# Moving scan work and one filler unit around the seams of a two-layer DiT kernel on one core

## The chip, the cores and the metric

The kernel runs on one core of a Trainium2 chip, in one launch. Five engines work side by side, each through its own queue in order: TensorE (PE; its weight loads are listed as PEld), VectorE (DVE), ScalarE (ACT), GpSimd (POOL) and SyncE (SP), which issues DMAs here; POOL issues DMAs too. The metric is the device time of one execution in microseconds; the median of several runs counts.

## The reference

One sequence of 256 tokens (`x`) and a context of 256 tokens (`ctx`), both 2048 wide, go through two layers in float32. All 18 arrays are inputs; the weights are read from memory once per run.

```python
h = _rmsnorm(x, norm_g[i]) * (1 + scale) + shift          # shift, scale, gate = silu(c) @ ada_w[i] + ada_b[i]
# layer 0: Fourier mixer, for x and for ctx
u, z = jnp.split(h @ w_in, 2, axis=-1)                    # 2 x 4096 wide
f = jnp.fft.fft2(ug, axes=(1, 3), norm='ortho').real      # 16 groups of 256
y = einsum('bngc,gcd->bngd', f, w_mix) * silu(z)
# layer 1: attention of x over itself and ctx
q, k, v, z = jnp.split(h @ w_in, [4096, 4608, 5120], axis=-1)   # 64 query heads, 8 key/value heads of 64
s = (q @ k.T) * 64 ** -0.5, masked to a window of 128, plus all of ctx
p = softmax(concat([s, sink]))[..., :-1]
y = (p @ v) * silu(z)
# both layers
x = x + gate * (y @ w_out[i])
# at the end
out = _rmsnorm(x, final_g)
```

## The kernel before

Products are made at nearly float32 accuracy from pairs: a value is split into a high part (a cast on ACT) and a low part (a subtraction on DVE or POOL), and `mm3` (lines 145 to 147) issues three matmuls, high by high, high by low and low by high. Two kinds of pairs are used, f16 (`split16`, lines 137 and 138) and fp32r (`split`, lines 66 and 67). The f16 kind needs scale factors so that nothing overflows; they are taken from sums of squares of the weights. For that reason the kernel reads the later weights ahead, in pieces of 128x1024 (512 KB), and squares and sums each piece, while earlier stages run. "Scan" means this reading and squaring in what follows.

The stages, in the order of time: the opening (norm and transform of x, and adaLN products) and the Fourier groups; the z product of layer 0 (32 blocks); layer 0's output product, a loop of 32 tiles (`i`, two sweeps of 16 for the two halves of the columns), in which the remaining adaLN sums are made on DVE too; norm and keys and values of layer 1 (8 weight blocks `kg`); the attention loop; and the output product of layer 1 with the final norm.

The pools that matter: `raw` (3 slots of 1 MB for weights as they land), `ws` (6 slots for split weights), `act` (33 slots of 128x512 float32), and 8 banks of PSUM, `ps`. A pool `kvp` lives through the keys' and values' stage; the pool `at` of the attention loop opens when it has closed. `h1` has 16 slots for layer 1's input and, later, for the parts of its output y.

The scan in layer 0's output product. `scan_loads1(n)` (called with `w_rate[i]` at tile `i`) issues n pieces, each as two loads of 256 KB into `act` slots, on POOL's queue (line 821 holds such a load). `scan_sums()` squares on ACT (line 829) what is pending, at the next tile. At tile 28 `h1_bound()` reduces the sums that the scale factors of the next stage need, and turns them through memory (two small DMAs on POOL); `h1_scale()` at tile 31 makes the factors. At tiles 12 to 15 and 28 to 31 POOL also loads x for the residual, and POOL's queue then holds the constants of layer 1: rope, mask and sinks (line 60). `ada_rate` gives the number of adaLN steps a tile takes.

The scan in the keys' and values' stage. `loads2(n)` issues pieces into four slots `pz` of `kvp`, 35 in all, over steps 0 to 11 (two steps per weight block); `sums2()` (lines 1177 and 1179) squares what is pending on ACT or on DVE. A last `sums2(True)` takes what is left once the stage's products are out of PSUM, and line 1235 reduces the 35 sums into one. The products leave PSUM through copies on ACT (1224 and 1225 for the values and their absolute values, 1231 for the context's keys) and the rotation on DVE (`roped`, 1132 to 1138). The values' own scale comes from a small product of ones with their absolute values (line 1238), then lines 1240 to 1254 make the f16 pair of the values: a product on DVE (1252), a cast on ACT (1253), a subtraction on POOL (1254).

The attention loop. All weight products of layer 1's queries, z and the first of its output rows are cut into units of one 128x1024 half block: 8 units for each of 8 groups of query heads ("q"), 2 for each of 32 z blocks ("z"), and 14 "o" units, each two of the 32 steps of k of the first 512 output columns. `emit_unit()` prepares the weights of the next unit and issues the products of the current one; `filler()` calls it and may issue a postponed transposition of queries. 10 units come ahead of the loop. Then, for each head `i`: scores, mask and softmax (`stage_s`, 1489 to 1509; the mask and the maximum are one DVE instruction, line 1491; the high and low f16 parts of the probabilities are lines 1506 on ACT and 1507 on DVE; DMAs on SP's queue transpose them, line 1509), a filler, the product with the values of head `i - 2` (`stage_o`, 1524 and 1525), and another filler. The last o steps, k = 28 to 31, are left for `first_rest()` in the stage after the loop, and the parts of y for them lie in the pool `fin`.

What sets the order. Tile's planner goes over the whole program once, simulates the engines, and writes each engine's queue: among the instructions that are ready by its own times it takes the one that the program names first. Program order is thus a priority and not the order itself. `tc.issue_after(x)` ties what stands inside it behind x on x's engine.

Of the kernel before, what the change touches and what calls it, by code (L numbers as in the profile page):

```python
# [11 lines left out]
F32R = mybir.dt.float32r  # L12
F16 = mybir.dt.float16
AF = mybir.ActivationFunctionType
ALU = mybir.AluOpType
AX = mybir.AxisListType

P = 128
# [3 lines left out]
NB = DB // P  # L22
# [10 lines left out]
def tile_dit(ctx: ExitStack, tc: tile.TileContext, a: dict, out: bass.AP):  # L33
    nc = tc.nc
    V, S, PE, GP = nc.vector, nc.scalar, nc.tensor, nc.gpsimd
# [8 lines left out]
    def psum():  # L44
        return pp.tile([P, 512], F32, tag="ps", name="ps")
# [9 lines left out]
    def act(dt=F32):  # L55
        return actp.tile([P, 512], dt, tag="act", name="act")
# [8 lines left out]
    def split(h, l, src, eng=V):  # L65
        last_cast[0] = S.copy(h, src).ins  # L66
        last_sub[0] = eng.tensor_tensor(l, src, h.bitcast(F32), op=ALU.subtract).ins  # L67
# [76 lines left out]
    def mm3(o, wh, wl, xh, xl, start, stop):  # L144
        PE.matmul(o, wh, xh, start=start, stop=False)  # L145
        PE.matmul(o, wh, xl, start=False, stop=False)  # L146
        return PE.matmul(o, wl, xh, start=False, stop=stop).ins  # L147
# [491 lines left out]
    for g in range(G):  # L639
        for j in {13: (8, 9), 14: (10, 11)}.get(g, (g - 5,) if 5 <= g < 13 else ()):  # L640
            t = up.tile([P, 1024], F32, name="pz", tag="pz", bufs=1)
# [164 lines left out]
    scn = adat.tile([P, 108], F32, name="scn")  # L806
# [5 lines left out]
    yq = adab[:, 1, 0].rearrange("p k s -> p (k s)")  # L812
# [46 lines left out]
    with tc.tile_pool(name="yp", reuse_waits="tile", bufs=32) as ypool:  # L859
        ys = []  # L860
# [38 lines left out]
        if True:  # L899
# [21 lines left out]
            for kg in range(4):  # L921
# [10 lines left out]
                for j in range(4):  # L932
                    k = kg * 4 + j
# [66 lines left out]
        identr = act(F32R)[:, 0:P]  # L1000
        S.copy(identr, ident)
        ada_rate = {**{i: 2 for i in (*range(6, 10), *range(17, 26))}, **{i: 0 for i in (14, 15, 16, 28, 29, 30, 31)}}
        w_rate = {10: 1, 11: 1, 14: 2, 15: 2, 16: 2, 17: 1, 18: 1, 20: 1, 22: 1, 24: 1, 26: 2, 27: 2, 28: 3, 29: 2, 30: 1}
        hbd = dram.tile([P, 2], F32, name="hbd")
        hb1 = []

# [24 lines left out]
        for i in range(32):  # L1031
# [26 lines left out]
            if kg >= 12:  # L1058
                for k in range(sw * 8 + (kg - 12) * 2, sw * 8 + (kg - 12) * 2 + 2):
                    t = act()  # L1060
# [79 lines left out]
    with tc.tile_pool(name="h1", reuse_waits="tile", bufs=16) as h1p:  # L1140
# [4 lines left out]
        with tc.tile_pool(name="kvp", reuse_waits="tile", bufs=2) as kvp:  # L1145
# [4 lines left out]
            for k in range(KT):  # L1150
                z2 = kvp.tile([P, 1024], F16, tag="hz", name="hz", bufs=16)
                t = kvp.tile([P, 512], F32, tag="ht", name="ht")
# [18 lines left out]
            scn = kvp.tile([P, 35], F32, name="scn", bufs=1)  # L1171

            def sums2(act_only):
                for n in range(len(pend)):
                    t, c = pend.pop(0)
                    if n < 2 or act_only:
                        S.activation(t, t, AF.Square, accum_out=c)
                    else:
                        V.tensor_tensor_reduce(t, t, t, 1.0, 0.0, ALU.mult, ALU.add, c)
# [16 lines left out]
            for kg in range(8):  # L1196
# [16 lines left out]
                for j in range(2):  # L1213
                    k = kg * 2 + j
# [7 lines left out]
            for tb in range(4):  # L1222
                t, ab = act(), act(F32R)
# [3 lines left out]
                t = act()  # L1227
# [3 lines left out]
                    S.activation(t, o[tb][0], AF.Copy, scale=dnk)  # L1231
                kr.append(t)

            sums2(True)
            V.tensor_reduce(yq[:, 17:18], scn, axis=AX.X, op=ALU.add)
            l1 = psum()
            for tb in range(4):
                PE.matmul(l1, oner, vs[tb][1], start=tb == 0, stop=tb == 3)
# [9 lines left out]
            for tb in range(4):  # L1248
                t = vs[tb][0]
                va = actp.tile([P, 8, P], F16, tag="act", name="v")  # L1250
                tv = t.rearrange("p (h d) -> p h d", d=64)
                V.tensor_tensor(t, t, up_, op=ALU.mult)
                S.copy(va[:, :, 0:64], tv)
                GP.tensor_tensor(va[:, :, 64:128], tv, va[:, :, 0:64], op=ALU.subtract)
                v01.append(va)

        y1 = []
        raw1, fin = [None], []
        oA, kg1, yh = [], [0], []
        with tc.tile_pool(name="at", reuse_waits="tile", bufs=2) as at:  # L1260
# [4 lines left out]
            def w1_next():  # L1265
                n = kg1[0]
                kg1[0] += 1
                if n % 2 == 0:
                    raw1[0] = raw(a["wo1a"][n // 2])
                return half_split(raw1[0], n % 2)  # L1270

            def y_split(k):
                t = (h1p if k < 28 else fin[0]).tile([P, 512], F32R, tag="h1" if k < 28 else "ys", name="ys", bufs=16 if k < 28 else 4)
                split(t[:, 0:N], t[:, N : 2 * N], y1[k // 2][:, (k % 2) * N : (k % 2 + 1) * N], GP if k < 24 else V)
                yh.append(t)

# [3 lines left out]
            def y_sums(n, i):  # L1280
                while ynext[0] < min(n, len(ypairs)) and ypairs[ynext[0]] <= i - 2:
                    j = ynext[0]
                    ynext[0] += 1
                    S.activation(act(), y1[j], AF.Square, accum_out=yq[:, j : j + 1])

            def out_scale():
                V.tensor_reduce(yq[:, 18:19], yq[:, 0:14], axis=AX.X, op=ALU.add)
                o = psum()
                for c, i, st in ((0, 16, True), (0, 17, False), (1, 18, True)):
                    PE.matmul(o[:, c : c + 1], ones.broadcast_to([P, P]), yq[:, i : i + 1], start=st, stop=i > 16)  # L1290
                V.tensor_scalar(yq[:, 28:30], o[:, 0:2], 2.0**-70, None, op0=ALU.max)
                V.tensor_scalar(yq[:, 20:22].bitcast(I32), yq[:, 28:30].bitcast(I32), 24, 23, op0=ALU.logical_shift_right, op1=ALU.logical_shift_left)
                V.tensor_scalar(yq[:, 22:24].bitcast(I32), yq[:, 20:22].bitcast(I32), -1.0, 204.0 * 2**23, op0=ALU.mult, op1=ALU.add)
                V.tensor_tensor(ub, uw, uy, op=ALU.mult)
                V.tensor_scalar(dn1.bitcast(I32), yq[:, 20:21].bitcast(I32), yq[:, 21:22].bitcast(I32), -27.0 * 2**23, op0=ALU.add, op1=ALU.add)
# [18 lines left out]
                return h, l  # L1314

            def o1_step(k, os_, wh, wl):
                while len(yh) <= min(k + 4, NB - 1) and (len(yh) < 28 or fin):
                    y_split(len(yh))
                for tb in range(2):
                    mm3(os_[tb], yh[k][:, tb * P : (tb + 1) * P], yh[k][:, N + tb * P : N + (tb + 1) * P], wh, wl, k == 0, k == NB - 1)  # L1320
# [58 lines left out]
            def units():  # L1379
                order = [("q", 0)]  # L1380
                for hk in range(8):
                    if hk < 7:
                        order.append(("q", hk + 1))
                    order += [("z", b) for b in range(hk * 4, hk * 4 + 4)]
                for kind, n in order:
                    if kind == "q":
                        oq = []
                        for kg in range(4):
                            for i in range(2):
                                yield kind, n, kg * 2 + i, oq  # L1390
                    else:
                        oz = []
                        for i in range(2):
                            yield kind, n, i, oz
                for k in range(14):
                    yield "o", k, 0, None

            ulist = list(units())
# [113 lines left out]
            def stage_t(ft, fs):  # L1512
                for tb in range(2):
                    o = pp.tile([P, 8, P], F16, tag="ps", name="ps")
                    for j in range(8):
                        PE.transpose(o[:, j, :], fs[tb][:, j * P : (j + 1) * P], ident16[0])
                    (S.copy if tb == 0 else V.tensor_copy)(ft[:, :, tb, :], o)
# [30 lines left out]
            def filler():  # L1548
                j = slot[0]
                slot[0] += 1  # L1550
                emit_unit()
                if defer and defer[0][0] + 2 < j:
                    defer.pop(0)[1]()

            pts = {}
            for i in range(66):
                if i % 8 == 0:
                    while defer:
                        defer.pop(0)[1]()
                if i == 61:  # L1560
                    t = actp.tile([P, 1024], F16, tag="act", name="ident16")
                    ident16.append(t[:, 0:P])
                    S.copy(ident16[0], ident)
                y_sums(14, i if i < 60 else 99)
                if i == 62:
                    out_scale()
                if i < 64:
                    pts[i] = stage_s(i)
                if i - 2 >= 61:
                    stage_t(*pts[i - 2])  # L1570
                filler()
                if i >= 2:
                    stage_o(i - 2, *pts.pop(i - 2))
                filler()


        with tc.tile_pool(name="fin", reuse_waits="tile", bufs=1) as fp:
# [30 lines left out]
                    y_half(j)  # L1608

            def first_rest():  # L1610
                for k in range(28, NB, 2):
                    w = w1_next()
                    for i in range(2):
                        o1_step(k + i, oA, *(t[:, i * 512 : (i + 1) * 512] for t in w))
                S.activation(gbc[:, 512:], gbc[:, 512:], AF.Copy, scale=dn1)
                for tb in range(2):
                    evac(tb, 0, oA[tb])

            o = [[psum() for _ in range(2)] for _ in range(2)]
            for kg in range(16):  # L1620
                if kg == 2:
                    first_rest()
                t = raw(a["wo1b"][kg])
# [7 lines left out]
                for j in range(2):  # L1631
                    k = kg * 2 + j
# [43 lines left out]
            for kg in range(8):  # L1676
                t = raw(a["wo1c"][kg])
# [136 lines left out]
```

## Time and profile before

| | |
|---|---|
| median of three runs | 1768.69 us (1767.99 to 1774.59) |
| the profiled execution | 1770.58 us, span 1768.8 us |
| PE busy | 1728.3 us, 98% |
| DVE busy | 1426.8 us, 81% |
| ACT busy | 1151.0 us, 65% |
| POOL busy | 362.2 us, 20% |
| read from memory | 422.45 MB, 246 GB/s over the span |
| granted clock of TensorE, mean | 0.997 |

A row of a timeline reads: start and duration in us, engine, line, operation, what it writes and from what, shapes, how many instructions were merged, and in brackets how long the engine had been idle and what ended that. An engine's name with a q is its queue, where DMAs are issued. A row of waits reads: who waited for whom, us in total, how often, the longest. A row of stretches gives the busy time of each engine in that stretch (and its instructions), then the granted clock of TensorE, the busy share of the DMA engines and the rate in GB/s. PE's busy time counts a pipelined matmul from start to end, so a busy PE is one that has work, not one at its peak.

### The profile page before, as it was taken

To read this page: it belongs to the slowest core of one execution; us is meant where nothing else is said; L and a number is where in the kernel's file an instruction comes from. 1 tells how busy PE (TensorE), PEld (TensorE's weight loads), DVE (VectorE), ACT (ScalarE), POOL (GpSimd) and SP (SyncE) were. 2 spreads that over 40 slices of the span, in tenths; PEclk is the share of its full clock that TensorE was granted. 3 is DMA by queue.
4 is the path that set the end of the run, shared out by engine and by line. 5 is a ranking of instruction groups with operands and counts; after the bars stand their busy time and mean duration, and the time that the engine had idled before them with its cause. 6 is when DMAs were issued, how large, how long until landed. Compare 5 with 4: busy or idle time off the path is not lost. (4 is left out here: it accounts for less than half of the span.)

```text
span 1768.8 us, 26913 instructions
## 1 busy us (share of the span) xinstructions
PE 1728.3 (98%) x9539; PEld 1143.4 (65%) x9539; DVE 1426.8 (81%) x2489; ACT 1151.0 (65%) x2199; POOL 362.2 (20%) x489
## 2 busy tenths in 40 slices
PE   6999999999999999999999998999999999999998
PEld 4679999644444444446444645788888888887454
DVE  5779889797677786877697685899899899998755
ACT  5545556477777755466224685788888788898643
POOL 0002111212222214212211211422213212251001
PEclk9999999999999999999999999999999999999999
DMA  9998998778988969977986696578888887878653
GB/s 394 417 357 247 278 278 251 290 286 315 332 306 315 313 225 367 357 284 259 373 316 212 213 363 217 176 195 214 209 200 211 213 208 202 206 196 286 218 186 119
DMA packets 233127, 468.80 MB, mean 265 GB/s; under 512 B 154560, under 2 KB 154960, under 8 KB 206112
## 3 DMA queue, kind: packets, MB, share of 16 engines
q1 hardware_dynamic: 180672, 331.41, 58.0%
q0 software_dynamic: 48176, 128.72, 22.8%
q10 hardware_dynamic: 4144, 6.95, 1.2%
q8 instruction: 75, 1.23, 0.3%
q14 instruction: 60, 0.49, 0.1%
HBM read 422.45 MB, written 12.59 MB: 246 GB/s over the span
## 5 line engine op out<-in xcount | busy, mean ns | idle before, releaser
L67 DVE TENSOR_TENSOR wl<-raw,wh 128x1024 fp32r<-128x1024 f32 x152 | 201.4, 1326 | 40.3 <-ACT wh L66 37.3
L146 PE MATMUL ps<-act,wf 128*128 128x512 f16 x512 | 194.0, 379 | 0.0
L147 PE MATMUL ps<-act,wf 128*128 128x512 f16 x512 | 191.1, 379 | 0.0
L145 PE MATMUL ps<-act,wf 128*128 128x512 f16 x512 | 189.8, 379 | 0.6
L1451 PE MATMUL ps<-h,wh 128*128 128x512 f32 x512 | 184.8, 397 | 0.0
L66 ACT CAST wh<-raw 128x1024 fp32r<-128x1024 f32 x152 | 158.2, 1041 | 27.6 <-PE ps L146 18.8
L145 PE MATMUL ps<-y,wf 128*128 128x512 f16 x448 | 169.8, 379 | 0.8 <-ACT wf L137 0.8
L146 PE MATMUL ps<-y,wf 128*128 128x512 f16 x448 | 169.8, 379 | 0.0
L147 PEld LDWEIGHTS <-wf 128*128 128x128 f16 x960 | 93.8, 98 | 113.2
L145 PEld LDWEIGHTS <-wf 128*128 128x128 f16 x960 | 93.7, 98 | 113.2 <-ACT wf L137 4.2
L147 PE MATMUL ps<-y,wf 128*128 128x512 f16 x448 | 166.5, 379 | 0.0
L146 PEld LDWEIGHTS <-wf 128*128 128x128 f16 x960 | 93.9, 98 | 109.1
L137 ACT ACTIVATE wf<-raw,nrm 128x1024 f16<-128x1024 f32 x56 | 63.5, 1145 | 134.7 <-PE ps L147 77.4
L1453 PE MATMUL ps<-h,wl 128*128 128x256 f32 x512 | 138.7, 281 | 0.3 <-DVE wl L67 0.3
L829 ACT ACTIVATE act<-act 128x512 f32<-128x512 f32 x174 | 107.1, 616 | 20.2 <-DMA act<-in_wo1b 13.5
L1494 ACT ACTIVATE p<-ps,mx 128x512 f32<-128x512 f32 x128 | 88.1, 689 | 40.5 <-DVE mx L1491 36.3
L138 DVE SCALAR_TENSOR_TENSOR wf<-raw,tn,wf 128x1024 f16<-128x1024 f32 x64 | 79.8, 1281 | 41.9 <-ACT wf L137 41.8
L790 POOL DMA_DIRECT2D wa<-in_adw x64 | 34.0, 532 | 387.5 <-PE ps L147 125.1
L1507 DVE SCALAR_TENSOR_TENSOR f<-p,sm,f 128x512 f16<-128x512 f32 x128 | 103.6, 835 | 8.4 <-ACT f L1506 8.0
L1451 PEld LDWEIGHTS ps<-h,wh 128*128 128x128 f32 x512 | 96.2, 188 | 18.9
L1506 ACT ACTIVATE f<-p,sm 128x512 f16<-128x512 f32 x128 | 87.7, 717 | 26.6 <-DMA ft<-f 16.0
L146 PE MATMUL ps<-wl,h 128*128 128x512 f32 x256 | 102.5, 401 | 0.5 <-DVE wl L67 0.4
(424 smaller groups left out, 4873.0 us busy)
## 6 DMA issues: line engine op xcount, KB each, us to landing
raw<-in_wz SPq DMA_DIRECT2D x64, 1024.0 KB, 5.9
raw<-in_awp SPq DMA_DIRECT2D x32, 1024.0 KB, 12.9
zr<-in_adw SPq DMA_DIRECT2D x64, 512.0 KB, 6.9
wa<-in_adw POOLq DMA_DIRECT2D x64, 512.0 KB, 6.5
act<-in_wo POOLq DMA_DIRECT2D x128, 256.0 KB, 7.6
raw<-in_wo SPq DMA_DIRECT2D x32, 1024.0 KB, 8.3
raw<-in_wq SPq DMA_DIRECT2D x32, 1024.0 KB, 5.3
raw<-in_wu SPq DMA_DIRECT2D x32, 1016.0 KB, 6.8
```

Source lines behind the costliest of these rows:

```text
L66: last_cast[0] = S.copy(h, src).ins
L67: last_sub[0] = eng.tensor_tensor(l, src, h.bitcast(F32), op=ALU.subtract).ins
L138: last_sub[0] = V.scalar_tensor_tensor(w[:, 1], src, up, w[:, 0], op0=ALU.mult, op1=ALU.subtract).ins
L145: PE.matmul(o, wh, xh, start=start, stop=False)
L146: PE.matmul(o, wh, xl, start=False, stop=False)
L147: return PE.matmul(o, wl, xh, start=False, stop=stop).ins
L829: S.activation(t, t, AF.Square, accum_out=c)
L1451: PE.matmul(o[0], wh[:, q], hx1[k], start=k == 0, stop=k == KT - 1)
L1453: PE.matmul(o[0][:, 0:N], wl[:, q], hx1[k][:, 0:N], start=False, stop=False)
L1494: S.activation(pt[tb], so[tb], AF.Exp, bias=mx[:, tb : tb + 1], scale=-1.0, accum_out=sm[:, tb : tb + 1])
L1506: fa = S.activation(f[:, 0:512], pt[tb], AF.Copy, scale=sm[:, tb : tb + 1]).ins
L1507: f_last[:] = fa, V.scalar_tensor_tensor(f[:, 512:1024], pt[tb], sm[:, tb : tb + 1], f[:, 0:512], op0=ALU.mult, op1=ALU.subtract).ins
```

## The change

Three places are touched, with what follows from them.

- `w_rate`: the 23 pieces of layer 0's output product are spread otherwise. Tile 24 issues 2 instead of 1, tiles 26 and 27 issue 3 instead of 2, tile 28 still 3, tiles 29 and 30 none instead of 2 and 1.
- The last `sums2(True)` and the reduce of the 35 sums move from ahead of the ones product (line 1238) to behind the values' pairs, and are tied behind the last value's cast on ACT (line 1253), whose instruction is now kept in `last_v`.
- In the attention loop head 1 gets a third filler, ahead of its second one (heads 0 and 1 have no `stage_o`). The units needed for it come from a fifteenth o unit: k = 28 and 29 are taken in the loop, their parts of y lie in `h1` instead of `fin`, and `first_rest()` begins at k = 30.

```diff
-        w_rate = {10: 1, 11: 1, 14: 2, 15: 2, 16: 2, 17: 1, 18: 1, 20: 1, 22: 1, 24: 1, 26: 2, 27: 2, 28: 3, 29: 2, 30: 1}
+        w_rate = {10: 1, 11: 1, 14: 2, 15: 2, 16: 2, 17: 1, 18: 1, 20: 1, 22: 1, 24: 2, 26: 3, 27: 3, 28: 3}
...
-            sums2(True)
-            V.tensor_reduce(yq[:, 17:18], scn, axis=AX.X, op=ALU.add)
+            last_v = []
             l1 = psum()
...
-                S.copy(va[:, :, 0:64], tv)
+                last_v[:] = [S.copy(va[:, :, 0:64], tv).ins]
                 GP.tensor_tensor(va[:, :, 64:128], tv, va[:, :, 0:64], op=ALU.subtract)
                 v01.append(va)
+            with tc.issue_after(last_v[0]):
+                sums2(True)
+                V.tensor_reduce(yq[:, 17:18], scn, axis=AX.X, op=ALU.add)
...
-                t = (h1p if k < 28 else fin[0]).tile([P, 512], F32R, tag="h1" if k < 28 else "ys", name="ys", bufs=16 if k < 28 else 4)
+                t = (h1p if k < 30 else fin[0]).tile([P, 512], F32R, tag="h1" if k < 30 else "ys", name="ys", bufs=16 if k < 30 else 4)
...
-                while len(yh) <= min(k + 4, NB - 1) and (len(yh) < 28 or fin):
+                while len(yh) <= min(k + 4, NB - 1) and (len(yh) < 30 or fin):
...
-                for k in range(14):
+                for k in range(15):
                     yield "o", k, 0, None
...
                 filler()
+                if i == 1:
+                    filler()
                 if i >= 2:
                     stage_o(i - 2, *pts.pop(i - 2))
                 filler()
...
-                for k in range(28, NB, 2):
+                for k in range(30, NB, 2):
```

## The prediction

> **What bounds the kernel now.** I read the page's first part, then the list of what TensorE (PE) waited for, then the stretches around each wait.
>
> ```profile
> span 1768.8 us, 26913 instructions
> PE 1728.3 (98%) x9539; PEld 1143.4 (65%) x9539; DVE 1426.8 (81%) x2489; ACT 1151.0 (65%) x2199; POOL 362.2 (20%) x489
> ```
>
> PE is busy for 1728.3 of 1768.8 us, so a change that removes no matmul can win at most the 40 us between, and only where PE sat idle. The waits of PE between 100 and 1300 us, and after 1500 us (us in total, times, longest):
>
> ```profile
> PE ps L1238 <- ACT act L1225: 4.9, 1, 4.9
> PE ps L1524 <- DMA ft<-f: 2.2, 2, 2.0
> PE ps L997 <- DVE act L991: 1.6, 1, 1.6
> ...
> PE ps L146 <- DVE wl L67: 1.8, 2, 1.6
> ```
>
> The longest is at L1238, the seam between the key/value product and the queries, and the change works on it. The timeline of PE there and at L1524, and the stretches around the seam (length; busy time of PE, PEld, DVE, ACT, POOL; clock; DMA share; GB/s):
>
> ```profile
> 1085.98 0.38 PE L147 MATMUL ps<-wf,hz 128*128 128x512 f16 x1
> 1091.25 0.80 PE L1238 MATMUL ps<-act,oner 128*128 128x512 f32 x1 [4.89 <-ACT act L1225]
> 1091.84 0.63 PE L145 MATMUL ps<-wh,h 128*128 128x512 f32 x1
> ...
> 1095.65 0.39 PE L145 MATMUL ps<-wh,h 128*128 128x512 f32 x1
> 1095.88 0.39 PE L146 MATMUL ps<-wl,h 128*128 128x512 f32 x1
> ...
> 1147.44 0.27 PE L1524 MATMUL ps<-ft,v 128*128 128x256 f16 x1 [2.02 <-DMA ft<-f]
> ...
> 1086.40:1088.70 2.30, 0.00 (x0) 0.00 (x0) 0.91 (x2) 0.57 (x1) 0.00 (x0) 1.00 0.96 397
> 1088.80:1091.20 2.40, 0.00 (x0) 0.00 (x0) 1.89 (x5) 2.40 (x6) 0.00 (x0) 0.50 0.07 31
> 1091.20:1095.60 4.40, 4.35 (x10) 3.47 (x11) 3.25 (x6) 4.08 (x8) 0.00 (x0) 0.50 0.00 0
> 1095.60:1098.00 2.40, 2.40 (x12) 1.89 (x11) 0.00 (x0) 0.00 (x0) 0.00 (x0) 1.00 0.03 7
> ```
>
> The stall costs twice. PE idles 4.89 us; 2.3 us into that the granted clock falls to 0.50 and stays there until 1095.6. Nine steps from 1091.84 to 1095.65 take 3.81 us, against 0.23 us a step afterwards (1095.65 to 1095.88), 2.1 us: 1.7 us lost, and 0.35 us more on the first product (0.59 instead of 0.24). So the seam costs 4.9 + 2.1 = 7.0 us.
>
> **The change, part by part.** First, the last squares. What ACT and DVE do at the seam:
>
> ```profile
> 1088.13 1.06 ACT L1177 ACTIVATE pz<-pz 128x1024 f32<-128x1024 f32 x1 [2.82 <-DMA pz<-in_wo1c]
> ...
> 1089.18 1.03 ACT L66 CAST wh<-raw 128x1024 fp32r<-128x1024 f32 x1
> 1090.12 0.57 ACT L1224 COPY act<-ps 128x512 f32<-128x512 f32 x1
> 1090.60 0.60 ACT L1225 ACTIVATE act<-ps 128x512 fp32r<-128x512 f32 x1
> ...
> 1087.23 0.08 DVE L1179 DVE_READ_ACCUMULATOR2_ANT scn<- 128x1 f32 x1
> 1089.31 0.19 DVE L1235 TENSOR_REDUCE adab<-scn 128x1 f32<-128x35 f32 x1 [2.00 <-ACT pz L1177]
> 1089.42 0.68 DVE L1132 TENSOR_TENSOR act<-ps,act 128x512 f32<-128x512 f32 x1
> 1090.01 0.74 DVE L1137 TENSOR_TENSOR rt<-ps,act 128x256 f32<-128x256 f32 x2
> ```
>
> ACT stands 2.82 us in one square of a weight piece whose DMA lands at 1088.1, with the cast of the next query weights and the copies that PE wants queued behind it. DVE waits 2.00 us in the reduce that reads that square's sum, with the keys' rotation (L1132) behind it. loads2 issues 35 pieces, the last at step 11 after that step's squares, so one square is left for this place; the change puts it and the reduce behind the last value copy (L1253).
>
> Without the square ACT was idle from 1085.3 (1088.13 − 2.82), so the cast (1.03 us) fits before PE ends at 1086.36, and the first copy starts at about 1086.5 instead of 1090.12. From copy to L1238 took 1.13 us (1090.12 to 1091.25), so L1238 goes at about 1087.6. The query products also need free banks. The keys and values hold all 8, and the first bank that ACT frees goes to L1238 itself. DVE frees the next: it is held until 1087.31 by its own square (not moved), then needs the 1.33 us from 1089.42 to 1090.75: 1088.6. ACT's second pair is done about then too, a second copy and L1225 after the first pair's 1.1 us. So the queries start at 1088.65 instead of 1091.84: 3.2 us. PE then idles some 1.3 + 0.8 = 2.1 us with a product between, like the 2.02 us at L1524, after which matmuls kept their full pace. I take the clock as kept: the 1.7 us of the nine steps more (the 0.35 us lie ahead of 1091.84 and are in the 3.2). Term: −4.9 us; ends −7.0 (stall and slow stretch vanish) and −1.0 (banks come late and the clock falls all the same).
>
> [...]
>
> The square and its reduce do not vanish: 1.06 us plus its read on ACT and 0.19 us on DVE now stand ahead of the copies of the turned keys. Their cover:
>
> ```profile
> 1112.72 8.41 POOL L1346 TENSOR_TENSOR kkl<-act,kkh 64x512 fp32r<-64x512 f32 x4 [0.50 <-PE ps L146]
> ...
> 1135.29 0.40 PE L1489 MATMUL ps<-kkh,qa 128*128 128x512 f32 x1
> ```
>
> The keys' low parts are done at 1121.1, the first scores come at 1135.3: 14 us of room for 1.3 us. Without that cover the price would be 1.3 us; I take 0.
>
> Second, the extra filler at head 1. Program order was masks of head 2, unit 14, values of head 0 (L1524), unit 15; it becomes unit 14, masks of head 2, unit 15, values of head 0, unit 16. Around the 2.02 us wait (DVE, then ACT, then SP's queue):
>
> ```profile
> 1139.41 0.76 DVE L1491 CUSTOM_DVE_ANT_0 ps<-ps,mask,nsink 128x512 f32<-128x512 f32 x1
> ...
> 1140.08 0.16 DVE L1497 RECIPROCAL sm<-sm 128x2 f32<-128x2 f32 x1
> ...
> 1141.95 1.41 DVE L1507 SCALAR_TENSOR_TENSOR f<-p,sm,f 128x512 f16<-128x512 f32 x2
> 1143.51 1.23 DVE L67 TENSOR_TENSOR wl<-raw,wh 128x1024 fp32r<-128x1024 f32 x1
> ...
> 1140.62 1.33 ACT L1506 ACTIVATE f<-p,sm 128x512 f16<-128x512 f32 x2
> ...
> 1142.77 2.72 SPq L1509 DMA_TRANSPOSE ft<-f  x2
> ```
>
> The third head's mask at 1139.41 stands between the first head's sum and its reciprocal, and a second mask follows. Two such masks are 1.4 us ahead of the low parts (L1507), whose end at 1143.4 lets SP's second transposition go; PE gets the data at 1147.44. ACT's high parts (L1506) start at 1140.62 and hold the low parts, so of the 1.4 us I count about half to all. But the order on PE is the planner's, made by its own times: an earlier head 0 may also be put earlier among the units, and then the wait stays. Against that, the weights of the unit after 15 were split by 1144.65 (L67), before PE ran dry at 1145.42 (1147.44 − 2.02), so there was work to put there. Term: −1.0 us, between 0 and −2.0.
>
> The unit itself is moved, not added: twelve products of 0.23 us (2.8 us), one cast and one subtraction of 1024 columns, two splits of y. It leaves the final stage and makes the loop longer by as much, so 0 if both stay bound by PE. The loop's end is the place to watch (stretches with the same columns):
>
> ```profile
> 1500.00:1550.00 50.00, 49.65 (x288) 41.65 (x287) 46.57 (x89) 41.54 (x85) 10.79 (x8) 1.00 0.86 212
> 1550.00:1600.00 50.00, 47.93 (x257) 39.02 (x256) 47.46 (x88) 45.44 (x103) 25.99 (x26) 1.00 0.77 199
> 1593.78 0.50 PE L146 MATMUL ps<-wl,ys 128*128 128x512 f32 x1 [1.58 <-DVE wl L67]
> ```
>
> There DVE sets the pace, and DVE's part of the unit (a 1.2 us subtraction and two short ones, about 2 us in all) comes into it. SP's queue gets the load of the eighth weight block before the final stage's first blocks instead of after two of them. I take +0.3 us, between −1 and +2.
>
> Third, the pieces. Three of 512 KB, six loads and six squares, leave tiles 29 and 30 for 24, 26 and 27.
>
> ```profile
> 966.79 2.12 POOL L821 DMA_DIRECT2D act<-in_wo1b  x4
> ...
> 980.98 0.54 POOL L60 DMA_DIRECT2D sink<-in_sink  x1
> ...
> 987.21 0.19 DVE L1126 TENSOR_SCALAR nsink<-sink 128x64 f32<-128x64 f32 x1 [1.28 <-DMA sink<-in_sink]
> ...
> 863.55 1.28 DVE L138 SCALAR_TENSOR_TENSOR wf<-raw,nrm,wf 128x1024 f16<-128x1024 f32 x1 [5.03 <-ACT wf L137]
> ...
> 850.00:860.00 10.00, 10.00 (x48) 4.47 (x46) 1.86 (x3) 0.00 (x0) 3.22 (x6) 1.00 1.02 400
> ```
>
> At the old place the loads sat among POOL's loads of x and of the next stage's constants. The sinks, issued at 980.98, reach DVE at 987.21; it waits 1.28 us for them amid the evacuation that makes PE wait 1.56 us at L997. With 1.5 MB less in flight they may land sooner. At the new place the loads join a burst that already fills the DMA engines (share 1.02, 400 GB/s): 1.5 MB at that rate is 3.9 us, in front of the loads of adaLN weights (wa) behind them on POOL and beside SP's. DVE already idles 5.03 us there for weights while PE is busy 10.00 of 10 us, so I cost it at 0; without that cover it is up to +3.9. The six squares land on an ACT that is busy 0.0 of those 10 us. Term: −0.3 us, between −1.6 and +3.9.
>
> **Sum.** −4.9 − 1.0 + 0.3 − 0.3 = −5.9 us. The profiled execution took 1770.58 us (span 1768.8); minus 5.9 is 1764.7. The median of the three runs, 1768.69, lies 1.9 below it, so I forecast 1762.8.
>
> **The rivals.** (a) All waits named go: 7.0 + 2.0 + 1.6 = 10.6 us, 1758.1. For it: each has its part of the change. Against: banks bind next at the seam, DVE's own late square keeps it busy to 1087.3. (b) The stall merely shrinks: the clock falls nevertheless or the banks come in another order, −2.5 us, 1766.2. For it: the fall after 2.3 us, when 2.1 remain. (c) No gain: the planner, which orders all engines anew, puts another late item in the square's place (DVE's square or the weight cast), or the loads of the pieces starve PE for what the seam gives: 1768.7, give or take 2. (d) Slower: in the loop every head now stands one unit later against the weights. DVE is busy 46.57 of 50 us there, and 64 heads from 1135.3 to about 1600 are 7.3 us each, so DVE has 0.5 us to spare per head. If the new phase makes PE wait 0.3 us more per head, that is 62 × 0.3 = 18.6 us less the 5.9: 1781. It decides from 0.1 us per head up. Against it: PE lost only 0.35 us in the whole stretch from 1500 to 1550, and units a step ahead are ready sooner, not later.
>
> **How the numbers follow.** Forecast as summed (about 1760 to 1766): 0.57. (a) 0.14, (b) 0.12, (c) 0.10, (d) 0.07. 0.5% is 8.8 us, about what a measurement of this kernel can tell from no change. Faster than 1759.8: (a) and the forecast's low edge, 0.17. Slower than 1777.5: (d), 0.07. The rest, 0.76, lies between. The range takes in the forecast, (a), (b) and most of (c): 1757 to 1770, leaving out (d) and edges.
>
> **What would show it.** Right: at L1238 less than 2.5 us of idling, the granted clock at 1.00 through the seam, the L1177 square after L1253, DVE's rotation right behind its own square, and the L1524 wait near 1 us. Wrong: a clock of 0.50 at the seam; a new wait of PE between 860 and 960 us; a longer one than 1.58 us before the loop's end; or PE's busy share from 1150 to 1550 below 49 of 50 us.

## The result, and the profile after

The changed kernel takes 1781.82 us (median of five, 1779.54 to 1784.71); the kernel before 1771.42 (median of five). The ratio is 1.0061, with a 95% interval of 1.0042 to 1.0081: slower by 10.4 us, where 5.9 us less were forecast. In the experiment with the weight loads on ACT's queue the profiled execution ran at a mean granted clock of 0.944 and took 1825.09 us; it is left out of that experiment's median below, and of its trace only what the DMAs did is read. The profiled execution of after took 1784.71 us, the slowest of its five; its span is 14.1 us longer than that of before (1782.9 against 1768.8), and these 14.1 us are what the traces can account for. Line numbers in the loop are two higher than before (L1524 is L1526, L1509 is L1511), the ones product is L1237.

The first part of the page, after:

```profile
span 1782.9 us, 26857 instructions
PE 1730.0 (97%) x9539; PEld 1145.4 (64%) x9539; DVE 1442.0 (81%) x2489; ACT 1149.3 (64%) x2199; POOL 362.3 (20%) x489
```

PE's busy time has hardly changed (1728.3 before), so the loss is waiting. Where it lies is seen in one long stretch of the attention loop, in both kernels (columns: length; busy time of PE, PEld, DVE, ACT, POOL; granted clock; DMA share; GB/s). Before:

```profile
1150.00:1580.00 430.00, 427.81 (x2358) 355.14 (x2358) 399.34 (x745) 357.75 (x722) 103.76 (x77) 1.00 0.85 207
```

After:

```profile
1150.00:1580.00 430.00, 412.04 (x2259) 342.39 (x2258) 398.97 (x715) 341.44 (x688) 88.70 (x62) 0.99 0.82 201
```

PE idles 2.2 us there before and 18.0 us after; DVE does as much in both, and the DMA engines move no more. What PE waited for between 1150 and 1650 us (total, times, longest), before:

```profile
PE ps L146 <- DVE wl L67: 2.2, 3, 1.6
PE ps L1524 <- DMA ft<-f: 1.0, 3, 0.6
```

and after:

```profile
PE ps L1526 <- DMA ft<-f: 17.5, 12, 4.9
PE ps L1526 <- DVE wf L138: 1.5, 1, 1.5
PE ps L146 <- DVE wl L67: 1.1, 1, 1.1
PE ps L1526 <- ACT p L1496: 0.5, 1, 0.5
```

One wait went from 1.0 to 17.5 us: the product with the values (L1526) waits for the DMAs that transpose the probabilities, not for weights. These waits recur with the key/value groups of eight heads: six of the twelve, with 12.8 of the 17.5 us, are at the heads 5 mod 8 (13, 21, 29, 37, 45, 53), the others one to three heads behind these (23 with 1.8 us, and 32, 38, 39, 40 and 48). Head 45 shows how. Before, its first score, the last of its low parts on DVE, SP's queue, and its first product with the values:

```profile
1466.41 0.49 PE L1489 MATMUL ps<-kkh,qb 128*128 128x512 f32 x1
...
1481.11 0.74 DVE L1507 SCALAR_TENSOR_TENSOR f<-p,sm,f 128x512 f16<-128x512 f32 x1
...
1476.57 0.33 SPq L50 DMA_DIRECT2D raw<-in_wq  x1
1480.19 2.92 SPq L1509 DMA_TRANSPOSE ft<-f  x2
...
1485.49 0.28 PE L1524 MATMUL ps<-ft,v 128*128 128x256 f16 x1
```

and the same head after:

```profile
1474.02 0.48 PE L1491 MATMUL ps<-kkh,qb 128*128 128x512 f32 x1
...
1489.78 1.41 DVE L1509 SCALAR_TENSOR_TENSOR f<-p,sm,f 128x512 f16<-128x512 f32 x2
...
1489.90 0.33 SPq L50 DMA_DIRECT2D raw<-in_wq  x1
1490.61 4.91 SPq L1511 DMA_TRANSPOSE ft<-f  x2
...
1498.28 0.27 PE L1526 MATMUL ps<-ft,v 128*128 128x256 f16 x1 [2.26 <-DMA ft<-f]
```

The DMA issues of these two moments (how many, size, median us from issue to landing), before (1480 to 1482.5 us) and after (1489.8 to 1493 us):

```profile
ft<-f SPq DMA_TRANSPOSE x2, 3.1
```

```profile
raw<-in_wq SPq DMA_DIRECT2D x1, 1024.0 KB, 5.8
ft<-f SPq DMA_TRANSPOSE x2, 6.2
```

Before, PE had 19.1 us of other work between the scores and the values of head 45 (1466.41 to 1485.49, no wait), and the low parts were done 15.4 us after the scores; the transpositions took 3.1 us and landed at +18.6, half a microsecond early. After, the extra unit gives PE more work in between (24.3 us less the wait of 2.3 is 22.0), but the low parts end at +17.2, and SP issues a load of 1 MB 0.7 us ahead of the first transposition. The transpositions then take 6.2 us and land at +24.2. At head 53, just ahead of the last z blocks, the extra work is missing (18.8 us between scores and values), and the wait is 4.87 us; 2.6 us into it, at 1558.59 us, the granted clock fell to 0.50 again (stretches of after):

```profile
1556.00:1560.80 4.80, 0.03 (x1) 0.00 (x0) 4.05 (x11) 3.65 (x7) 0.00 (x0) 0.77 1.11 278
1560.90:1565.40 4.50, 4.50 (x17) 3.68 (x18) 3.73 (x8) 4.39 (x11) 0.00 (x0) 0.50 1.04 285
```

The seam did get better, though by less than forecast. Timeline of PE, ACT and DVE there after, and the stretch behind it:

```profile
1086.60 0.49 PE L1237 MATMUL ps<-act,oner 128*128 128x512 f32 x1 [1.39 <-ACT act L1225]
1088.14 0.76 PE L145 MATMUL ps<-wh,h 128*128 128x512 f32 x1 [1.04 <-DVE rt L1137]
...
1083.48 1.06 ACT L1177 ACTIVATE pz<-pz 128x1024 f32<-128x1024 f32 x1 [2.67 <-DMA pz<-in_wo1c]
...
1085.49 1.23 DVE L1179 CUSTOM_DVE_ANT_0 pz<-pz 128x1024 f32<-128x1024 f32 x1 [4.67 <-DMA pz<-in_wo1c]
...
1087.60:1090.90 3.30, 2.76 (x7) 2.21 (x8) 3.27 (x8) 3.02 (x6) 0.00 (x0) 0.50 0.12 51
```

PE idles 1.39 + 1.04 = 2.43 us instead of 4.89. The clock fell all the same, for 3.41 us instead of 6.83; work at half pace from 1088.14 to 1090.96 costs 1.4 us instead of 2.1. So the seam costs 3.8 us instead of 7.0.

The account against before, in the two profiled executions: loop to 1580 us +15.8 (18.0 less 2.2), the slow clock behind head 53 +2.3 (half of 1560.90 to 1565.42), the loop's end +1.0 (1.08 + 1.47 instead of 1.58), seam −3.2, first product with values −0.5 (1.49 instead of 2.02), the ones product L997 −1.4 (0.20 instead of 1.56). That is +14.0, of 14.1 measured.

### The profile page after: what moved, and what is told of

It is laid out like the page before. It is cut to its first block, busy times and chain, and to the rows that moved or that the text cites. A ratio compares the mean times of both kernels' runs of the same rounds, so it can differ in the third digit from the quotient of the medians.

```text
span 1782.9 us, 26857 instructions
## 1 busy us (share of the span) xinstructions
PE 1730.0 (97%) x9539; PEld 1145.4 (64%) x9539; DVE 1442.0 (81%) x2489; ACT 1149.3 (64%) x2199; POOL 362.3 (20%) x489
## 5 line engine op out<-in xcount | busy, mean ns | idle before, releaser
L145 PE MATMUL ps<-act,wf 128*128 128x512 f16 x512 | 189.8, 379 | 0.6 <-ACT wf L137 0.2
L145 PE MATMUL ps<-y,wf 128*128 128x512 f16 x448 | 169.8, 379 | 0.8 <-ACT wf L137 0.8
L145 PEld LDWEIGHTS <-wf 128*128 128x128 f16 x960 | 93.7, 98 | 113.4 <-ACT wf L137 4.2
L1509 DVE SCALAR_TENSOR_TENSOR f<-p,sm,f 128x512 f16<-128x512 f32 x128 | 110.3, 888 | 13.2 <-ACT f L1508 12.8
L1453 PEld LDWEIGHTS ps<-h,wh 128*128 128x128 f32 x512 | 96.9, 189 | 19.1
## 6 DMA issues: line engine op xcount, KB each, us to landing
raw<-in_awp SPq DMA_DIRECT2D x32, 1024.0 KB, 12.7
```

The source lines that it names most:

```text
L1453: PE.matmul(o[0], wh[:, q], hx1[k], start=k == 0, stop=k == KT - 1)
L1509: f_last[:] = fa, V.scalar_tensor_tensor(f[:, 512:1024], pt[tb], sm[:, tb : tb + 1], f[:, 0:512], op0=ALU.mult, op1=ALU.subtract).ins
```

## The experiments

| what runs | median, us | ratio to before, 95% |
|---|---|---|
| squares and pieces, no extra unit | 1766.25 | 0.9957 to 0.9981 |
| extra unit alone | 1787.64 | 1.0077 to 1.0105 |
| all, head 3 gives the unit back | 1766.26 | 0.9957 to 0.9981 |
| all, weight loads on ACT's queue | 1789.73 | 1.0078 to 1.0113 |
| all, extra filler at head 41 | 1774.14 | 1.0010 to 1.0033 |
| all, extra filler at head 60 | 1765.13 | 0.9964 to 0.9984 |
| all, loads behind the late heads | 1784.39 | 1.0073 to 1.0099 |
| squares alone | 1763.35 | 0.9948 to 0.9974 |
| pieces alone | 1771.64 | 0.9990 to 1.0016 |
| one filler less, squares | 1793.06 | 1.0108 to 1.0143 |
| all but the pieces | 1783.96 | 1.0057 to 1.0086 |
| more squares late | 1766.60 | 0.9965 to 0.9985 |

"All" is the changed kernel. The kernel before had medians of 1770.5 to 1771.2 in the runs beside these.

**Which part loses.** Squares and pieces without the extra unit (the main lines, against the changed kernel):

```diff
-                for k in range(15):
+                for k in range(14):
...
-                if i == 1:
-                    filler()
```

> Before, with the moved squares and the moved pieces, but without the extra filler and without the fifteenth o unit. Theory 1 (the extra unit puts the attention loop out of step, so that weight loads land in front of late heads' transpositions): the loop waits as little as before (under 8 us of PE in all after 1140 us) and the seam's gain stays, so 3 to 6 us faster than before. Theory 2 (the loop went wrong because the earlier parts let it start at another moment against the DMAs): slower than before by 8 to 14 us. Theory 3 (only the end of the loop is hurt, by the o unit there): 3 to 6 us faster, like theory 1.

and the extra unit without them (against the kernel before):

```diff
+                if i == 1:
+                    filler()
...
-                for k in range(14):
+                for k in range(15):
```

> Before, with the extra filler at head 1 and the fifteenth o unit alone. Theory 1: 13 to 18 us slower than before, with PE waits of 1 to 2.3 us at the heads 13, 21, 29, 37, 45 and 53. Theory 2: within 2 us of before. Theory 3: 6 to 9 us slower, with the waits only after head 52.

The first is 4.5 us faster than before, the second 16.9 us slower; in it the waits for the transpositions stand as in after (PE's waits between 1160 and 1580 us):

```profile
PE ps L1524 <- DMA ft<-f: 15.1, 9, 4.0
```

The loss is the extra unit's, and the earlier start of the loop, which squares and pieces bring too, has no part in it.

**Is it the step, or the unit?** All of the change, but head 3 issues one filler less and there are 14 o units. The mask of head 2 still goes behind the unit at head 1:

```diff
                 if i == 1:
                     filler()
...
-                filler()
+                if i != 3:
+                    filler()
```

> The moved squares and pieces, the extra filler at head 1, but head 3 has one filler fewer, and there are fourteen o units as before: from head 4 on the units stand to the heads as before the change. Theory 1: the loop's waits as before (under 8 us after 1140 us), 3 to 7 us faster than before. Theory 2: 8 to 14 us slower. Theory 3: 3 to 6 us faster. If an early shift alone is enough to upset the loop (a fourth way), some 5 us slower or more, with the waits at the heads 5 mod 8 again.

1766.26 us, and no wait of PE between 1150 and 1580 us above 0.6 us. What costs is not the added filler at head 1 but that all later heads stand one unit further on in the row of loads.

**Where the step is taken.** The extra filler at head 41, with the fifteenth unit and all else as in after:

```diff
-                if i == 1:
+                if i == 41:
                     filler()
```

> The changed kernel with its extra filler at head 41 instead of head 1; fifteenth o unit, squares and pieces stay. Theory 1 (from the extra filler on, the loads of weights meet the transpositions of every head 5 mod 8): heads 13, 21, 29 and 37 keep the fast phase and do not wait, so of the 22 us of waits in the loop only those of head 45 and later stay, about 10 to 12 us (head 53 among them); time 1766.3 (squares and pieces alone) plus 6 to 10, so 1772 to 1776. Theory 2 (the loop's end alone, where the fifteenth unit is): all of the loss stays, 1780 or more. Theory 3 (the masks of head 2 at head 1, and what follows from them in the first heads): no loss, 1766.

1774.14 us. PE's waits for the transpositions between 1150 and 1480 us, and from 1480 to 1650 us:

```profile
PE ps L1526 <- DMA ft<-f: 0.6, 2, 0.4
...
PE ps L1526 <- DMA ft<-f: 7.4, 3, 4.8
```

Heads 13 to 37 are as fast as before; the waits begin at head 45 (0.8 us), and the 4.8 us are head 53's. The same at head 60:

```diff
-                if i == 1:
+                if i == 60:
                     filler()
```

> The changed kernel with its extra filler at head 60 instead of head 1, so that the fifteenth o unit is in the loop but all heads to 59 keep their phase. Theory 1 (phase): no waits over 0.6 us between 1150 and 1580 us, 1765 to 1768, as with squares and pieces alone. Theory 2 (the loop's end with a fifteenth unit): a wait of 3 us or more near 1560 to 1650 us and 1772 or more.

1765.13 us, no wait above 0.6 us from 1150 to 1580 us: the fifteenth unit at the loop's end costs nothing. The loss grows with the number of groups that stand out of step.

**One step in the other direction.** Squares moved, thirteen o units, and head 1 with one filler:

```diff
-                filler()
+                if i != 1:
+                    filler()
```

> The squares moved, the pieces as before, and head 1 with one filler instead of two (thirteen o units in the loop): the loop is one unit out of step in the other direction. Theory 1 (the phase decides which transpositions have a load beside them): the late heads and the loads stand in a third arrangement; PE's waits in the loop are somewhere else than at heads 5 mod 8 with 21.7 us of work ahead of them. If the fast phase is the only good one, 1770 to 1780; if only the step forward is bad, 1763 to 1766. Theory 2 (less work ahead of a head's values is always worse, more always better): the step back gives less lead and more waits, above 1770.

1793.06 us, the slowest of all. PE's waits between 1160 and 1580 us:

```profile
PE ps L1526 <- DMA ft<-f: 21.1, 18, 4.0
```

Sixteen of the eighteen stand at heads 6, 7 and 0 mod 8, which are now the late ones with a load beside them; two are at heads 25 and 33, and heads 5 mod 8 have none. Of the two neighbouring phases neither is good; 1770 to 1780 was expected for that, so the size was missed. Not all of the loss is the phase's: head 1, whose values now come one filler sooner, waits 4.3 us for its transposition, where it waits in no other version.

**The load beside the transposition.** If a load of 1 MB makes the transposition late, one that comes behind it must not. In after, the load that the program asks for at each head 0 mod 8 is tied behind the second transposition of the head 5 mod 8:

```diff
+                    hold = tie[0] and at_head[0] % 8 == 0 and tied[0] != at_head[0]
+                    with tc.issue_after(tie[0]) if hold else nullcontext():
                         raws1[src] = raw(a["wq"][n, i // 2] if kind == "q" else a["wz1"][n])
...
+                        tr = nc.sync.dma_start_transpose(ft[:, :, tb, :], f).ins
+                        if i % 8 == 5:
+                            tie[0] = tr
```

> The changed kernel with the first load of weights asked for in the program at each head 0 mod 8 tied behind the second transposition of the head 5 mod 8 that stands beside it on SP's queue. Theory 1a (the transpositions of those heads are late because a load of 1 MB is in flight): theirs take 3.1 to 3.6 us from issue to landing instead of 5.4, land at about +21 us after the head's scores instead of +23.5, and PE's waits there of 1.2 to 2.3 us fall below 0.5; the time falls to 1768 to 1775, unless the tied load makes the next unit's weights late. Theory 1b (the later reciprocal and low parts on DVE are the cause and the load adds nothing): the landing comes at +22 us or later all the same, the waits stay above 1 us, 1780 or more.

1784.39 us, so the time did not fall; but the heads in question did what the theory said. Head 45 on SP's queue, and its first product with the values:

```profile
1491.79 2.62 SPq L1516 DMA_TRANSPOSE ft<-f  x2
1494.45 1.06 SPq L50 DMA_DIRECT2D raw<-in_wq  x2
1497.28 0.33 SPq L50 DMA_DIRECT2D raw<-in_wz  x1
...
1498.16 0.28 PE L1533 MATMUL ps<-ft,v 128*128 128x256 f16 x1
```

The transpositions now took 3.2 us and landed 20.1 us after the scores, and PE did not wait; heads 21, 29, 37 and 53 landed after 19.7 to 20.4 us, and neither they nor head 13 made PE wait. The waits moved to other heads (most at 2 and 3 mod 8, with 19, 26, 27, 35, 42 and 43 among them; the longest is head 54's), whose transpositions now have loads ahead of them, and sum up to as much (1160 to 1580 us):

```profile
PE ps L1533 <- DMA ft<-f: 17.7, 14, 3.5
```

So without the load these heads are not late, and a load that is moved falls on others. The load alone does not make a head late, though. Before, 35 of the 42 heads from 16 to 57 had a load with 2 us or more to go when their second transposition was issued, and PE waited 1.0 us in all for these: their low parts were done 10.0 to 13.7 us after the scores, and the data landed after 16.4 to 19.5 us. The heads 5 mod 8 had their low parts at 15.0 to 16.1 us, and no load. After, fewer heads have a load (18 of the 42), but at the heads 5 mod 8 it meets low parts that end at 16.8 to 17.3 us, and they land at 23.1 to 24.2 us, with 22.0 us of PE work ahead of them, or 18.8 at head 53. In these traces it takes both, late low parts and a load. Why the low parts are late at these heads was not looked into.

**Is it SP's queue?** On SP's queue the transposition is issued behind the load. The loop's loads of query and z weights, but for the first of them, on ACT's queue instead:

```diff
-                    raws1[src] = raw(a["wq"][n, i // 2] if kind == "q" else a["wz1"][n])
+                    raws1[src] = raw(a["wq"][n, i // 2] if kind == "q" else a["wz1"][n], nc.scalar if n > (1 if kind == "q" else 3) else None)
```

> The changed kernel, with the loop's weight loads issued from ACT's queue instead of SP's; the transpositions stay alone on SP's queue. If a transposition takes 5 to 6 us because it stands in line behind a 1 MB load on SP's queue: it lands in 3.0 to 3.7 us from issue everywhere, head 45's about 20.5 us after its scores against 21.7 us of PE work, so the waits at the heads 5 mod 8 go and the kernel is 6 to 14 us faster than the changed one. If the two share the DMA engines whatever the queue: landing stays at 5 to 6 us beside a load, time within 3 us of the changed kernel. If ACT is held up by loads that wait for a free slot: slower than the changed kernel, with ACT idle ahead of line 50.

1789.73 us, 7.9 above the changed kernel. Within 3 us of it was expected for the case that queues make no difference, so this was missed too. A transposition issued behind a load on ACT's queue that had 3.2 us or more to go, longer than a transposition takes alone, took 6.2 us (median of 37), and one with no load in flight 3.2 us (of 39); in after, on one queue, it is 6.0 us (of 44) and 3.1 us (of 39). Standing behind the load on one queue is thus not needed for the delay. What it comes from instead, no run shows.

There is a new loss as well. At heads 15, 31 and 47 the second transposition is issued 0.44 us ahead of a load on ACT's queue, and yet lands half a microsecond behind it (head 15, issues between 1277.5 and 1278 us):

```profile
raw<-in_wz ACTq DMA_DIRECT2D x1, 1024.0 KB, 9.8
ft<-f SPq DMA_TRANSPOSE x1, 10.7
```

The three take 10.7 to 11.2 us. On SP's queue a load 1.3 us or more behind a transposition left it at 3.1 to 3.2 us in before; a load that close behind does not occur there.

**The seam and the pieces alone.** The squares and nothing else:

```diff
-            sums2(True)
-            V.tensor_reduce(yq[:, 17:18], scn, axis=AX.X, op=ALU.add)
...
+            with tc.issue_after(last_v[0]):
+                sums2(True)
+                V.tensor_reduce(yq[:, 17:18], scn, axis=AX.X, op=ALU.add)
```

> The kernel before with the last squares and their reduce moved, and nothing else. By the two traces the wait at the seam falls from 4.89 to 2.43 us and the slow clock behind it is 3.4 us shorter, which is half of that in time: 2.5 + 1.7 = 4.2 us, or 1766.5. If the pieces have a part in the 4.5 us that squares and pieces gave together (their wait of 1.56 us in layer 0's output product), 1767.5 to 1768.5. If the clock at the seam doesn't depend on the shorter wait, 1768.

1763.35 us, 7.1 below the kernel before: the lowest median here, and faster than both kernels. PE's waits between 1080 and 1150 us in it:

```profile
PE ps L1526 <- DMA ft<-f: 2.1, 1, 2.1
PE ps L145 <- DVE rt L1137: 0.8, 1, 0.8
```

The pieces and nothing else:

```diff
-        w_rate = {10: 1, 11: 1, 14: 2, 15: 2, 16: 2, 17: 1, 18: 1, 20: 1, 22: 1, 24: 1, 26: 2, 27: 2, 28: 3, 29: 2, 30: 1}
+        w_rate = {10: 1, 11: 1, 14: 2, 15: 2, 16: 2, 17: 1, 18: 1, 20: 1, 22: 1, 24: 2, 26: 3, 27: 3, 28: 3}
```

> The kernel before with the pieces of layer 0's output product at tiles 24 to 28 and nothing else. Theory A (the wait of 1.56 us at the ones product of layer 0's output product belongs to the old place of the pieces): the wait is gone, 1769 to 1769.5 against 1770.5. Theory B (that wait belongs to single executions, since the run with the squares alone and the one with the filler alone show 0.20 us there with the pieces at their old place): the same time within 0.5 us, or up to 3 us more, since squares with pieces took 1766.25 and squares alone 1763.35. The seam stays as before: some 4.9 us idle at the ones product of the values and a clock at half after it.

1771.64 us, the same as before (0.9990 to 1.0016). The seam was expected to stay as it was, some 4.9 us; in this trace ACT's last square waits 5.65 us for its load instead of 2.82, and PE idles 6.9 us at L1238 (5.7 with the extra unit alone). So the old seam's wait is not one number: it goes with when that load lands. And the changed kernel without them:

```diff
-        w_rate = {10: 1, 11: 1, ..., 22: 1, 24: 2, 26: 3, 27: 3, 28: 3}
+        w_rate = {10: 1, 11: 1, ..., 22: 1, 24: 1, 26: 2, 27: 2, 28: 3, 29: 2, 30: 1}
```

> The changed kernel with the pieces left at their old place. If the pieces cost what squares with pieces (1766.25) and squares alone (1763.35) differ by, 1779; if that difference was chance and the pieces do nothing, 1781 to 1783. The waits in the loop stay as in the changed kernel (about 20 us, the longest at head 53).

1783.96 us, 2.1 above the changed kernel, while squares with pieces took 2.9 more than squares alone. The two differences have opposite signs; whether the pieces do anything beside other parts stays open, but it is within 3 us. The 1.56 us at L997 are not theirs: that wait is 0.20 us in the profiles of the squares alone and of the extra unit alone, where the pieces are at their old place, and in that of the pieces alone; only the one execution of before that was profiled shows it.

**What is left at the seam.** Squares alone, with step 10's squares behind the values' copies as well:

```diff
-                            if kg * 2 + i < 12:
+                            if kg * 2 + i < 11:
                                 sums2(kg < 3)
```

> Squares moved and nothing else, and the squares of step 10 (two on ACT, one on DVE) go behind the values' copies too, so that no square that waits for a late load stands ahead of the seam's copies and rotation. Theory 1 (what is left of the wait at the seam, 0.8 to 2.9 us in the runs so far, is ACT's and DVE's last square waiting for their loads, which land at other times in each execution): less than 1 us idle at the seam, the clock stays at full there, and the time is 1761 to 1764. Theory 2 (the banks bind whatever the squares do): 1 to 2.5 us stay, 1763.4 as with the squares alone. If four squares on ACT are too many behind the values' copies: the first product with values waits longer than 2.1 us and the time is above 1764.

The wait at the seam is gone entirely:

```profile
1084.67 0.38 PE L147 MATMUL ps<-wf,hz 128*128 128x512 f16 x1
1084.70 0.58 PE L1237 MATMUL ps<-act,oner 128*128 128x512 f32 x1
1085.12 0.39 PE L145 MATMUL ps<-wh,h 128*128 128x512 f32 x1
```

but the time is 1766.60 us, above the 1764 that was the bound. Four squares stand on ACT one behind the other now, and casts of weights come late (PE's waits between 1090 and 1130 us, 1.6 of the 3.2 us by which this is slower than the squares alone):

```profile
PE ps L146 <- DVE wl L67: 0.8, 2, 0.5
PE ps L145 <- ACT wh L66: 0.8, 1, 0.8
```

So squares that waited for their loads were what still stood at the seam; the cost that was named for this case appeared, though not at the first product with values (1.99 us) but ahead of it.

## Why the prediction was wrong, point by point

- **The moved unit (+0.3, between −1 and +2).** This step failed. It costed the unit at 0 "if both stay bound by PE", looked for the price at the loop's end, and let rival (d) fall with "units a step ahead are ready sooner, not later". The extra unit alone costs 16.9 us in the runs. The unit's own work is hidden (0 at head 60); what isn't is the place of each head's work among the loads: late low parts and a load meet at the same heads. The prediction followed the weights, which PE never waited for between 1150 and 1580 us in after, and not the other transfer that SP's queue issues in the loop. The row was there, in the DMA issues of before between 1150 and 1650 us (median from issue to landing at its end):

```profile
ft<-f SPq DMA_TRANSPOSE x120, 5.1
```

  5.1 us was the usual time, but the transpositions of heads 37, 45 and 53 took 3.0 to 3.1 and landed only 0.5 to 0.8 us before PE came to their values. With 5.1 they would have been some 1.3 to 1.6 us late. Two of the signs of being wrong that were named did show: a clock of 0.50 at the seam, and PE busy 386.91 of 400 us between 1150 and 1550 us, which is 48.4 of 50.
- **Rival (d), 1781 us, chance 0.07.** It came near in time (1781.82) and in its price: 15.8 us over 62 heads is 0.25 us a head, where 0.3 was put down. That the time fits to 1 us is luck: it was 12.7 us above a kernel before of 1768.69, and the measured loss is 10.4 us above one of 1771.42. Its mechanism was half right: a new phase against the weights' loads, but through the transpositions and at a few heads of each group, not evenly through DVE. DVE did take part: its low parts at head 45 end 1.7 us later after the scores than before, and the landing is 5.6 us later.
- **The seam (−4.9).** Right in its cause and in the bank order: the rotation follows DVE's own square, and L145 waits for it; 1.3 + 0.8 us of idling were forecast, 1.39 + 1.04 measured. Mis-sized by the clock: it measured −3.2, which is the −4.9 without the 1.7 us that were put down for a clock that keeps its pace; it fell to 0.50 for 3.41 us. Squares alone got 0.8 us of idling and a granted clock of 1.00 there (1085.27 to 1088.50 us), and 7.1 us in time. What differs between the two executions is when the loads of the two squares that stay have landed: PE's last key/value product ends at 1085.2 or 1085.3 in both, and DVE's square starts at 1085.49 in after and at 1083.80 with squares alone.
- **The squares at their new place (0).** Right for one square: in after it runs at 1103.4 and nothing waits for it. Four of them cost 1.6 us (0.8 + 0.8): the 14 us of room were those of the keys, and the casts of weights on the same engine have less.
- **The third mask (−1.0).** The wait at the first product with values went from 2.02 to 1.49 us in after, and is 1.43 to 1.56 in the other runs with the filler at head 1, 1.95 to 2.08 in those without. So the sign was right and the size is −0.5.
- **The pieces (−0.3, up to +3.9).** Their loads did not starve PE between 860 and 960 us: PE is busy 100.00 of 100 us there. Alone they do nothing measurable.
- **The chances.** 0.07 for slower was too low: one row, the 0.5 to 0.8 us by which the late heads' transpositions land early, beside the 5.1 us that one usually takes, would have made (d) a case to reckon with.

## What to carry to other kernels

Where a loop of one period meets a stream of loads of another, a step of one unit can change which transfers meet, and which of them meet late work. Before you move a unit past such a loop, list for each kind of DMA that PE waits for how long before its use it lands, at the worst place of the period, and what a load ahead of it would add; a mean share of busy time shows none of that. And try the parts of a change one by one: here one part was worth −7.1 us and another +16.9.

## What the hardware did that was not expected

In before and after a transposition of 128x1024 f16 with no load of weights in flight at its issue took 3.1 us from issue to landing (median of 17 and of 39), and one issued behind a load of 1 MB landed about a microsecond behind that load: of 64 transpositions of before that were issued while a load had 3.2 us or more to go, so that they could have been first, none landed less than 0.87 us after it (median 1.06 us); of 44 in after none (0.85 and 1.04). With the loads on ACT's queue it was nearly the same: 37, none less than 0.63 us after it, median 1.05 us, read from that one trace. So there a queue of its own did not let a transposition land ahead of the load, nor did an issue 0.44 us earlier at heads 15, 31 and 47 (10.7 to 11.2 us). Why, no run here shows.

The granted clock fell in some waits of PE and behind some, and kept full in others. In the kernel before it was 0.50 for 6.83 us from 1088.78 us on, 2.4 us into the wait of 4.89 us at the seam. In after it was 0.50 for 3.41 us from 1087.55 us on, 0.45 us into the second of the two waits at the seam (1.39 and 1.04 us), and for 6.83 us from 1558.59 us on, 2.6 us into head 53's wait of 4.87 us; between the two it was 1.00, also behind head 45's wait of 2.26 us. Waits of nearly the same length differed from one execution to the next as well: the first product with values after 2.02 us in the kernel before kept full pace, and with the squares alone, after 2.08 us, it did not (0.22 us from one product to the next instead of 0.11):

```profile
1140.49 0.27 PE L1526 MATMUL ps<-ft,v 128*128 128x256 f16 x1 [2.08 <-DMA ft<-f]
1140.60 0.33 PE L1527 MATMUL ps<-ft,v 128*128 128x256 f16 x1
1140.72 0.42 PE L1526 MATMUL ps<-ft,v 128*128 128x256 f16 x1
1140.94 0.42 PE L1527 MATMUL ps<-ft,v 128*128 128x256 f16 x1
```

What decides whether a slow stretch follows a wait of about 2 us was not shown. For the forecast at the seam it was worth 1.7 us.
